# One-core two-layer trunk: the skip weights loaded as one row, a new order of the last rows, and three small moves in the projection blocks

## The chip, the cores and the metric

The kernel runs on one core of a Trainium2 chip. The metric is the device time of one execution in microseconds (us); lower is better. Five engines work side by side, each through its own instructions in program order: PE (TensorE, matrix products), DVE (VectorE), ACT (ScalarE), POOL (GpSimd) and SP (SyncE, which here only issues DMA transfers). They wait for each other through semaphores.

## The reference

The input is `x` of 1024 tokens by 1024 features, all float32. Two layers, each `h = h + W_out(mixer(rmsnorm(h)) * silu(z))`, then a last RMSNorm. Layer A mixes tokens within chunks of 128 by learned causal weights; layer B is a Mamba-2 state-space mixer with 32 heads. Cut to what matters here:

```python
def spatial_gating_mixer(h, w_in, ln_w, ln_b, w_s, b_s, w_out):     # layer A
    z, u, v = jnp.split(h @ w_in, 3, axis=-1)                       # 1024 -> 3 x 2048
    v = layernorm(v, ln_w, ln_b)
    mixed = jnp.einsum('gts,bcsgd->bctgd', w_causal, v) + b_s ...   # 8 groups, chunks of 128
    return (u * mixed * jax.nn.silu(z)) @ w_out

def ssd_mixer(h, w_in, conv_w, conv_b, dt_bias, a_log, d_skip, norm_w, w_out):   # layer B
    z, xbc, dt_raw = ...                                            # of h @ w_in
    xbc = silu(causal_depthwise_conv(xbc, conv_w, conv_b))
    dt = jax.nn.softplus(dt_raw + dt_bias)
    dA_cs = jnp.cumsum(dt * -jnp.exp(a_log), axis=2)
    ...                                                             # scan over 8 chunks
    y = y_diag + y_off + x * d_skip[..., None]                      # one skip weight a head
    gated = rmsnorm_by_group(y * jax.nn.silu(z))
    return gated @ w_out

h = h + mixer(rmsnorm(h, norm_w[i]), ...)                           # i = 0: A, i = 1: B
return rmsnorm(h, final_norm_w)
```

## The kernel before

Every large product is split into three products of rounded halves (`mm3`, lines 134 to 136: high by high, low by high, high by low), and two by two blocks of tokens and features are multiplied with seven block products in place of eight (Strassen's scheme, numbers 1 to 7 in the code). So weights have to be added to each other before they are used. ACT copies a sum into a rounded half `wh` or `xh` (line 111), DVE takes the rest into `wl` or `xl` (line 112), PE multiplies, and ACT copies some accumulators out (`u`, line 297). The order of all of this is written out by hand: the text of the program is the order on each engine. SBUF tiles come from small pools of a fixed number of buffers, taken in turn; who takes a buffer waits for its last user.

The run has these stages, with the times of the profile:

- Head (0 to about 190 us). `head()` normalises `x` and makes the first half of layer A's `v` columns, `rest()` the second half. Finished pieces of `v` lie in tiles `vt` of a pool of four 2 KB buffers (`k2`) and are stored to DRAM as `v_d` (line 397), by SP in the first half, by POOL in the second. Between them stand small loads on SP's queue: `hv` (lines 831 and 833, a bias and `a_log`) and the skip weights `dsk` (line 837), which layer B needs from about 1008 us on. `dsk` holds on partition `f * 64 + ...` the weights of the heads `2c + f`; the load takes every second weight of `b_d_skip`, once for each of 64 partitions. In `rest()`, `mix_a` masks layer A's mixing weights on POOL (line 861), `mix_b` transposes them on PE (869) and copies them on ACT into two `wc` tiles (871), which come from the same four `k2` buffers as `vt`, and `mix_c` multiplies `wc` by ones on PE (877).
- Layer A (to about 660 us): eight groups, then the output product.
- Projection blocks of layer B (about 640 to 1000 us): `into_b()` and `blocks()`. A block of 512 columns runs its seven products in units of 12 matmuls. `Block.sums_a` and `sums_b` build the two sums `t1` and `t2` in two halves of one tile: ACT writes minus a loaded block (lines 212, 218), and POOL's accumulating DMAs add further blocks from DRAM (line 203). `t2` feeds product 6, which comes third, and `fourth()` (line 228); `t1` feeds product 5, which comes fifth. Between the units stands `decays()`, a generator: each `yield` in it moves what follows to the next unit. It computes the time steps and their sums, with two exponentials on ACT (lines 1590 and 1620), stores them, spreads the last column of each chunk over 128 columns (`last`, line 1635), and has PE transpose them (1643) into `tk`.
- Scan and output product of layer B (about 1000 to 1447 us).
- End: `into_end()`. Rows of tokens are called (th, tt): th = 1 is the second half, ready first; th = 0 the first half, for which `last_mm(tt)` still runs 24 matmuls a row. `prep_unit` makes the operands of one `last_mm` (two `wh` on ACT, two `wl` on DVE). For a row of th = 0: `post` adds the product to the row on DVE (line 1232) and sums its squares on ACT (1251), `rstd_a` scales on DVE (1265) and takes a power on POOL (141), `rstd_b` refines on DVE (148, 152, 153), `finish_b` scales the left 512 columns on ACT (2201) and the right 512 on DVE (2203, together with the final norm weight `fnwb`), and two DMAs store them (2202, 2204). The left columns were weighed beforehand (2209).

Of the kernel before, what the change touches and what calls it, by code (L numbers as in the profile page):

```python
# [8 lines left out]
F32 = mybir.dt.float32  # L9
F32R = mybir.dt.float32r  # L10
AF = mybir.ActivationFunctionType
ALU = mybir.AluOpType
# [3 lines left out]
P = 128  # L16
# [13 lines left out]
def kernel(  # L30
# [21 lines left out]
    nc = tc.nc  # L52
    x = x[0]
    out = out[0]
# [3 lines left out]
    cst = ctx.enter_context(tc.tile_pool(name="cst", bufs=1))  # L58
# [6 lines left out]
    def s8(shape, name, dt=F32):  # L65
        return sb.tile(shape, dt, name=name, tag="s8", bufs=16)

    def q4(shape, name):
        return sb.tile(shape, F32, name=name, tag="q4", bufs=8)

    def k2(shape, name, dt=F32):
        return sb.tile(shape, dt, name=name, tag="k2", bufs=4)

    def k1(shape, name):
        return sb.tile(shape, F32, name=name, tag="k1", bufs=3)
# [21 lines left out]
    def sm(name):  # L97
        return ps[0].tile([P, 512], F32, name=name, tag="sm", bufs=n_sm[0])
# [84 lines left out]
    class Block:  # L183
# [32 lines left out]

        def sums_b(self):
            nc.scalar.mul(self.t1, self.b[0, 0], -1.0)
            self.add(self.t1, 0, 1)
            self.add(self.t2, 1, 1)  # L220

        def fourth(self):

# [604 lines left out]
    with tc.manual_schedule():  # L828
        second = head()
        hv = cst.tile([P, 4], F32, name="hv")  # L830
        nc.sync.dma_start(out=hv[0:32, 0:1], in_=b_dt_bias[0].rearrange("(h o) -> h o", o=1))
        for q in range(4):
            nc.sync.dma_start(out=hv[q * 32:(q + 1) * 32, 1:2], in_=b_a_log[0].rearrange("(h o) -> h o", o=1))
        dsk = cst.tile([P, 16], F32, name="dsk")
        dskv = b_d_skip[0].rearrange("(c f) -> f c", f=2)
        for f in range(2):
            nc.sync.dma_start(out=dsk[f * 64:(f + 1) * 64, :], in_=dskv[f].partition_broadcast(64))
        nA = hv[:, 2:3]
        nc.scalar.activation(nA, hv[:, 1:2], AF.Exp)
        nc.vector.tensor_scalar(nA, nA, -1.0, None, ALU.mult)  # L840
# [94 lines left out]
    for g in range(G):  # L935
        v = s8([P, NT, 256], "v")
# [645 lines left out]
    def decays():  # L1582

        dtw = q4([P, 4, 256], "dtw")
        cs = q4([P, 256], "cs")
        e_, s_, s2, p_ = (dtw[:, i, :] for i in range(4))
        V.scalar_tensor_tensor(e_, dtr, -1.0, dtr, ALU.mult, ALU.min)
        yield
        yield
        nc.scalar.activation(e_, e_, AF.Exp)  # L1590
        yield
        V.tensor_scalar(s_, e_, 2.0, None, ALU.add)
        V.reciprocal(s_[:, 0:P], s_[:, 0:P])
        yield
        V.reciprocal(s_[:, P:], s_[:, P:])
        V.tensor_tensor(s_, s_, e_, ALU.mult)
        V.tensor_tensor(s2, s_, s_, ALU.mult)
        yield
        V.tensor_scalar(p_, s2, 1.0 / 17, None, ALU.mult)
        for k in range(7, 0, -1):  # L1600
            if k in (5, 2):
                yield
            V.scalar_tensor_tensor(p_, p_, 1.0 / (2 * k + 1), s2, ALU.add, ALU.mult)
        V.scalar_tensor_tensor(p_, p_, 1.0, s_, ALU.add, ALU.mult)
        V.tensor_scalar(s2, dtr, 0.0, None, ALU.max)
        yield
        dt = dtr
        V.scalar_tensor_tensor(dt, p_, 2.0, s2, ALU.mult, ALU.add)
        dA = dtw[:, 0, :]
        V.tensor_scalar(dA, dt, nA, None, ALU.mult)  # L1610
        for j in range(2):
            V.tensor_tensor_scan(cs[:, j * P:(j + 1) * P], ones, dA[:, j * P:(j + 1) * P], 0.0, ALU.mult, ALU.add)
        yield
        dte = dtw[:, 2, :]
        for j in range(2):
            V.tensor_scalar(dte[:, j * P:(j + 1) * P], cs[:, j * P:(j + 1) * P], cs[:, j * P + P - 1:j * P + P], -1.0,
                            ALU.subtract, ALU.mult)
        yield
        ecs = dtw[:, 1, :]
        nc.scalar.activation(ecs, cs, AF.Exp)  # L1620
        nc.scalar.activation(dte, dte, AF.Exp)
        yield
        for q in range(4):
            rs_ = slice(q * 32, (q + 1) * 32)
            nc.gpsimd.dma_start(out=cs_d[2 * q:2 * q + 2].rearrange("c h l -> h c l"),
                              in_=cs[rs_, :].rearrange("h (c l) -> h c l", c=2))
            nc.gpsimd.dma_start(out=ecs_d[:, q * 256:(q + 1) * 256], in_=ecs[rs_, :])
            if q % 2:
                yield
        tk = s8([P, 2048], "tk")  # L1630
        tok = tk[:, 0:768].rearrange("p (v c r) -> p v c r", v=3, c=2)
        decb = tk[:, 768:1024]
        last = k1([P, 256], "last")
        for j in range(2):
            nc.scalar.copy(out=last[:, j * P:(j + 1) * P],
                           in_=ecs[:, j * P + P - 1:j * P + P].broadcast_to([P, P]))
        tps = []
        for two in ((dt, dte), (cs, last)):
            tp = sm("tp")
            tps.append(tp)  # L1640
            for i, src in enumerate(two):
                for j in range(2):
                    nc.tensor.transpose(out=tp[:, (2 * i + j) * P:(2 * i + j + 1) * P],
                                        in_=src[:, j * P:(j + 1) * P], identity=ident)
            yield
        nc.scalar.copy(out=tok[:, 0:2], in_=tps[0].rearrange("p (v c r) -> p v c r", v=2, c=2))
        yield
        nc.scalar.copy(out=tok[:, 2], in_=tps[1][:, 0:256].rearrange("p (c r) -> p c r", c=2))
        nc.scalar.copy(out=decb.rearrange("p (q j h) -> p j q h", q=4, j=2),
                       in_=tps[1][:, 256:512].rearrange("p (j q h) -> p j q h", j=2, q=4))  # L1650
        tok_of.update(tok=tok, decb=decb)
# [158 lines left out]
    def blocks():  # L1810
# [8 lines left out]
        bs[-1].apart = True  # L1819
        seq = [(k, n) for k in range(len(bs)) for n in (ORDER if k < len(bs) - 1 else LAST)]  # L1820
        small, turn, a21, done = decays(), [0], rest_a21(), []

        def ahead(at):
# [296 lines left out]
    def accs_b(n):  # L2120
        if n == 1:
# [3 lines left out]
    bo = Out(gd, b_w_out, gscale, lambda t, nb: h1_d[t][:, nb * 512:(nb + 1) * 512], accs_b, False,  # L2125
             (1, 2, 7, 6, 4, 5, 3))
    end = {}
# [68 lines left out]
            if c == 3:  # L2196
                bo.prep_unit(0)

    def finish_b(th, tt, rs):
        l, r = bo.row(th, tt, 0), bo.row(th, tt, 1)  # L2200
        nc.scalar.activation(l, l, AF.Identity, scale=rs)
        (nc.scalar if (th, tt) == (0, 3) else nc.sync).dma_start(out=outr[th * 4 + tt][:, 0:512], in_=l)
        nc.vector.scalar_tensor_tensor(r, r, rs, end["fnwb"][:, 512:], ALU.mult, ALU.mult)
        nc.sync.dma_start(out=outr[th * 4 + tt][:, 512:], in_=r)

    def weigh_left(th, t0):
        for tt in range(t0, t0 + 2):
            r = bo.row(th, tt, 0)
            nc.vector.tensor_tensor(out=r, in0=r, in1=end["fnwb"][:, 0:512], op=ALU.mult)  # L2209
# [221 lines left out]
    def into_end():  # L2431
        for n in (2, 7, 6, 4, 5):
            for _ in bo.product(n, hook_b):
                pass
        bo.prep_unit(1)
        weigh_left(1, 2)
        r1 = bo.rstd_half(1)
        for tt in range(4):
            bo.last_mm(tt)
            if 0 < tt < 3:  # L2440
                bo.prep_unit(tt + 1)
            if tt:
                bo.post(3, tt - 1)
                bo.rstd_a(0, tt - 1)
            finish_b(1, tt, r1[:, tt:tt + 1])
            if tt:
                finish_b(0, tt - 1, bo.rstd_b(0, tt - 1))
        bo.post(3, 3)
        bo.rstd_a(0, 3)
        finish_b(0, 3, bo.rstd_b(0, 3))  # L2450

    with tc.manual_schedule():
        scans()
        into_end()
# [28 lines left out]
```

## Time and profile before

| | us |
|---|---|
| median of 3 runs | 1481.93 (1481.75 to 1485.11) |
| the profiled execution | 1481.93 |
| its span, first to last instruction | 1480.2 |
| PE busy | 1452.0 (98%) |
| DVE busy | 1041.8 (70%) |
| ACT busy | 784.1 (53%) |
| POOL busy | 404.5 (27%) |

The profiled execution took the median's time; 1.73 us of it lie outside the span. Times in the profile count from the span's start. In a row of a timeline stand the start, the duration, the engine, the line, the operation with what it writes and reads, the count, and in brackets the engine's idle time before it with what ended that. PEq, SPq and so on are the sequencers that issue. In a list of waits stand who waited for whom, the sum in us, how often, and the longest.

### The profile page before, as it was taken

To read this page: it belongs to the slowest core of one execution; us is meant where nothing else is said; L and a number is where in the kernel's file an instruction comes from. 1 tells how busy PE (TensorE), PEld (TensorE's weight loads), DVE (VectorE), ACT (ScalarE), POOL (GpSimd) and SP (SyncE) were. 2 spreads that over 40 slices of the span, in tenths; PEclk is the share of its full clock that TensorE was granted. 3 is DMA by queue.
4 is the path that set the end of the run, shared out by engine and by line. 5 is a ranking of instruction groups with operands and counts; after the bars stand their busy time and mean duration, and the time that the engine had idled before them with its cause. 6 is when DMAs were issued, how large, how long until landed. Compare 5 with 4: busy or idle time off the path is not lost. (4 is left out here: it accounts for less than half of the span.)

```text
span 1480.2 us, 20005 instructions
## 1 busy us (share of the span) xinstructions
PE 1452.0 (98%) x7202; PEld 1196.5 (81%) x7202; DVE 1041.8 (70%) x1713; ACT 784.1 (53%) x1261; POOL 404.5 (27%) x451
## 2 busy tenths in 40 slices
PE   9998999999999999999999999999999999999997
PEld 7786888888888888887788888888888888787875
DVE  7864666776666655678665558767787777788976
ACT  7632333222323445565665646657677766866463
POOL 2101110000000023202122323205676767742221
PEclk9999999999999999999999999999999999999999
DMA  8653423332322999957467988786777566699963
GB/s 287 128 171 91 165 91 120 105 120 94 116 85 78 341 265 252 258 132 175 120 159 169 197 163 162 156 248 158 203 185 201 176 190 141 192 282 282 271 115 114
DMA packets 174549, 257.52 MB, mean 174 GB/s; under 512 B 16513, under 2 KB 98673, under 8 KB 171250
## 3 DMA queue, kind: packets, MB, share of 16 engines
q1 hardware_dynamic: 124128, 171.55, 37.7%
q0 software_dynamic: 42688, 70.79, 24.2%
q10 hardware_dynamic: 7634, 13.90, 2.6%
q8 instruction: 57, 0.93, 0.3%
q14 instruction: 42, 0.34, 0.1%
HBM read 187.19 MB, written 51.18 MB: 161 GB/s over the span
## 5 line engine op out<-in xcount | busy, mean ns | idle before, releaser
L134 PE MATMUL acc<-hh,wh 128*128 128x512 f32 x868 | 339.7, 391 | 0.7 <-ACT u L297 0.7
L136 PE MATMUL acc<-hh,wl 128*128 128x512 f32 x868 | 338.3, 390 | 0.4 <-DVE wl L112 0.3
L135 PE MATMUL acc<-hl,wh 128*128 128x512 f32 x868 | 337.8, 389 | 0.0
L136 PEld LDWEIGHTS acc<-hh,wl 128*128 128x128 f32 x868 | 162.9, 188 | 35.7 <-DVE wl L112 1.6
L134 PEld LDWEIGHTS acc<-hh,wh 128*128 128x128 f32 x868 | 163.1, 188 | 34.3 <-ACT u L297 1.1
L135 PEld LDWEIGHTS acc<-hl,wh 128*128 128x128 f32 x868 | 163.0, 188 | 33.0
L112 DVE TENSOR_TENSOR wl<-wr,wh 128x1024 fp32r<-128x1024 f32 (+1 forms) x81 | 96.2, 1188 | 105.8 <-ACT wh L111 105.6
L111 ACT CAST wh<-wr 128x1024 fp32r<-128x1024 f32 (+1 forms) x97 | 99.3, 1025 | 78.7 <-PE acc L135 58.7
L297 ACT COPY u<-acc 128x512 f32<-128x512 f32 x93 | 53.9, 582 | 148.0 <-PE acc L136 147.9
L134 PE MATMUL ab<-hh,wh 128*128 128x512 f32 x288 | 122.2, 424 | 0.0
L136 PE MATMUL ab<-hh,wl 128*128 128x512 f32 x288 | 113.2, 393 | 0.0
L135 PE MATMUL ab<-hl,wh 128*128 128x512 f32 x288 | 112.5, 391 | 0.6 <-DVE hl L112 0.6
L134 PE MATMUL acc<-wh,hh 128*128 128x512 f32 x216 | 85.6, 396 | 0.3 <-DVE vt L396 0.3
L135 PE MATMUL acc<-wl,hh 128*128 128x512 f32 x216 | 84.3, 390 | 1.0 <-DVE wl L364 1.0
L136 PE MATMUL acc<-wh,hl 128*128 128x512 f32 x216 | 84.1, 389 | 0.0
L976 POOL DMA_DIRECT2D y_d<-y x8 | 4.4, 550 | 287.2 <-DVE y L973 287.2
L1949 ACT ACTIVATE wl<-wl,tk 128x128 f32<-128x128 f32 x256 | 81.6, 392 | 0.3 <-DMA wl<-cs_d 0.2
L1967 DVE TENSOR_TENSOR wl<-wl,cw 128x512 f32<-128x512 f32 x64 | 61.0, 965 | 16.2 <-ACT wl L1951 15.1
L112 DVE TENSOR_TENSOR xl<-ya,xh 128x1024 fp32r<-128x1024 f32 x36 | 44.8, 1243 | 37.6 <-ACT xh L111 32.4
L1162 PE MATMUL bo<-wl,xh 128*128 128x512 f32 x192 | 64.2, 392 | 1.3 <-DVE stats L1253 0.7
L134 PEld LDWEIGHTS ab<-hh,wh 128*128 128x128 f32 x288 | 54.4, 189 | 13.3 <-issue 5.7
L111 ACT CAST xh<-ya 128x1024 fp32r<-128x1024 f32 x36 | 37.7, 1048 | 49.8 <-PE ao L1162 35.0
(331 smaller groups left out, 3236.4 us busy)
## 6 DMA issues: line engine op xcount, KB each, us to landing
wr<-in_a_w_in_dram SPq DMA_DIRECT2D x32, 512.0 KB, 3.6
wl<-cs_d SPq DMA_DIRECT2D x64, 256.0 KB, 5.4
wr<-in_b_w_in_dram SPq DMA_DIRECT2D x30, 512.0 KB, 4.3
wb<-in_a_w_out_dram SPq DMA_DIRECT2D x10, 1024.0 KB
wb<-in_b_w_out_dram SPq DMA_DIRECT2D x10, 1024.0 KB, 9.4
wr<-in_b_w_in_dram SPq DMA_DIRECT2D x36, 256.0 KB, 5.3
wide<-in_a_w_in_dram SPq DMA_DIRECT2D x16, 512.0 KB, 7.3
v<-v_d SPq DMA_DIRECT2D x8, 1024.0 KB
```

Source lines behind the costliest of these rows:

```text
L111: nc.scalar.copy(out=hi, in_=src)
L112: return (eng or nc.vector).tensor_tensor(out=lo, in0=src, in1=hi.bitcast(F32), op=ALU.subtract)
L134: nc.tensor.matmul(out=o, lhsT=l[0], rhs=r[0], start=start, stop=False, **kw)
L135: nc.tensor.matmul(out=o, lhsT=l[0], rhs=r[1], start=False, stop=False, **kw)
L136: nc.tensor.matmul(out=o, lhsT=l[1], rhs=r[0], start=False, stop=stop, **kw)
L297: nc.scalar.copy(out=self.u[n][:, i], in_=a)
L976: store = lambda: nc.gpsimd.dma_start(out=y_d[-1], in_=y)
L1162: nc.tensor.matmul(out=o[i], lhsT=X[x_][:, k, i * P:(i + 1) * P], rhs=Y[y_][:, k, :], start=not more and c == 0 and k == 0 and x_ == y_, s ...
L1949: nc.scalar.activation(wl[:, j, :], wl[:, j, :], AF.Relu, scale=-1.0, bias=tokc(2, c, self.g)[:, j:j + 1])
L1967: V.tensor_tensor(out=wl, in0=wl, in1=self.cw[c][:, 640:768].unsqueeze(1).broadcast_to([P, 4, P]), op=ALU.mult)
```

## The change

Five edits, in four places:

1. The skip weights come as one row of 32 values (`skip`, 128 bytes on each of 128 partitions) with one DMA in place of two, and DVE picks every second value with two copies of 64 partitions by 16.
2. `sums_b` adds to `t2` before it adds to `t1`.
3. In `decays()`, the first exponential (and all behind it) comes a unit later; the copies `last` stand a `yield` ahead of the transposes, which so come two units later than before.
4. The end is written out row by row: `prep_unit` comes ahead of the `finish_b` that stood before it, and `finish_b(1, 2)` after the sums of row (0, 1).
5. For the very last row the right half is weighed by `fnwb` (`left`) while the squares are summed, and DVE then only scales it.

```diff
@@ Block.sums_b
             nc.scalar.mul(self.t1, self.b[0, 0], -1.0)
+            self.add(self.t2, 1, 1)
             self.add(self.t1, 0, 1)
-            self.add(self.t2, 1, 1)
@@ behind head()
+        skip = cst.tile([P, 16, 2], F32, name="skip")
+        nc.sync.dma_start(out=skip.rearrange("p c f -> p (c f)"), in_=b_d_skip[0].partition_broadcast(P))
         dsk = cst.tile([P, 16], F32, name="dsk")
-        dskv = b_d_skip[0].rearrange("(c f) -> f c", f=2)
         for f in range(2):
-            nc.sync.dma_start(out=dsk[f * 64:(f + 1) * 64, :], in_=dskv[f].partition_broadcast(64))
+            nc.vector.tensor_copy(out=dsk[f * 64:(f + 1) * 64, :], in_=skip[f * 64:(f + 1) * 64, :, f])
@@ decays()
         yield
         yield
+        yield
         nc.scalar.activation(e_, e_, AF.Exp)
...
-        tk = s8([P, 2048], "tk")
-        tok = tk[:, 0:768].rearrange("p (v c r) -> p v c r", v=3, c=2)
-        decb = tk[:, 768:1024]
         last = k1([P, 256], "last")
         for j in range(2):
             nc.scalar.copy(out=last[:, j * P:(j + 1) * P],
                            in_=ecs[:, j * P + P - 1:j * P + P].broadcast_to([P, P]))
+        yield
+        tk = s8([P, 2048], "tk")
+        tok = tk[:, 0:768].rearrange("p (v c r) -> p v c r", v=3, c=2)
+        decb = tk[:, 768:1024]
@@ finish_b
-        nc.vector.scalar_tensor_tensor(r, r, rs, end["fnwb"][:, 512:], ALU.mult, ALU.mult)
+        if weighed is None:
+            nc.vector.scalar_tensor_tensor(r, r, rs, end["fnwb"][:, 512:], ALU.mult, ALU.mult)
+        else:
+            nc.vector.tensor_scalar(r, weighed, rs, None, ALU.mult)
@@ into_end()
-        for tt in range(4):
-            bo.last_mm(tt)
-            if 0 < tt < 3:
-                bo.prep_unit(tt + 1)
-            if tt:
-                bo.post(3, tt - 1)
-                bo.rstd_a(0, tt - 1)
-            finish_b(1, tt, r1[:, tt:tt + 1])
-            if tt:
-                finish_b(0, tt - 1, bo.rstd_b(0, tt - 1))
+        bo.last_mm(0)
+        bo.prep_unit(2)
+        bo.last_mm(1)
+        bo.post(3, 0)
+        bo.rstd_a(0, 0)
+        finish_b(1, 0, r1[:, 0:1])
+        bo.prep_unit(3)
+        finish_b(0, 0, bo.rstd_b(0, 0))
+        bo.last_mm(2)
+        bo.post(3, 1)
+        finish_b(1, 1, r1[:, 1:2])
+        bo.rstd_a(0, 1)
+        finish_b(1, 2, r1[:, 2:3])
+        finish_b(0, 1, bo.rstd_b(0, 1))
+        bo.last_mm(3)
+        bo.post(3, 2)
+        bo.rstd_a(0, 2)
+        finish_b(1, 3, r1[:, 3:4])
+        finish_b(0, 2, bo.rstd_b(0, 2))
         bo.post(3, 3)
+        left = k2([P, 512], "left")
+        nc.vector.tensor_tensor(out=left, in0=bo.row(0, 3, 1), in1=end["fnwb"][:, 512:], op=ALU.mult)
         bo.rstd_a(0, 3)
-        finish_b(0, 3, bo.rstd_b(0, 3))
+        finish_b(0, 3, bo.rstd_b(0, 3), left)
```

The engines' own order shows three of the places. In it the line numbers are those of each program; behind line 834 the changed one counts one to seventeen more.

SP's queue behind the last store of the first half, before, and then changed (`dsk` and `skip` are the skip weights; `64x16x1` is a transfer of single values):

```order
L863 DMA bsb<-in_a_b_s_dram 128x1024
L397 DMA v_d_79<-vt 256x1x256
L831 DMA hv<-in_b_dt_bias_dram 32x1
L833 DMA hv<-in_b_a_log_dram 32x1 x4
L837 DMA dsk<-in_b_d_skip_dram 64x16x1 x2
L937 DMA v<-v_d_78 128x2048
```

```order
L864 DMA bsb<-in_a_b_s_dram 128x1024
L397 DMA v_d_79<-vt 256x1x256
L831 DMA hv<-in_b_dt_bias_dram 32x1
L833 DMA hv<-in_b_a_log_dram 32x1 x4
L835 DMA skip<-in_b_d_skip_dram 128x32
L938 DMA v<-v_d_78 128x2048
```

Two transfers became one at the same place of the queue; the queue's other rows stand as they did. DVE's two copies of `skip` stand between the statistics of the second and the third piece of `v` of `rest()`.

ACT around the first exponential of `decays()` (`dtw`), before, and then changed:

```order
L297 COPY u<-acc 128x512
L1348 ACTIVATE zt<-zt 128x512
L1590 ACT_TABLE_LOAD
L1590 ACTIVATE dtw<-dtw 128x256
L111 CAST wh<-t_5546 128x1024
L297 COPY u<-acc 128x512 x2
L212 ACTIVATE t_5671<-wr 128x1024
```

```order
L297 COPY u<-acc 128x512
L1349 ACTIVATE zt<-zt 128x512
L111 CAST wh<-t_5548 128x1024
L297 COPY u<-acc 128x512
L1592 ACT_TABLE_LOAD
L1592 ACTIVATE dtw<-dtw 128x256
L297 COPY u<-acc 128x512
L212 ACTIVATE t_5670<-wr 128x1024
```

The table load and the exponential moved behind the cast `wh` and the first of the two copies `u`.

DVE in the end, from the norm of the second half (`rh`) to the finish of row (0, 0), before, and then changed (`wl` is `prep_unit`, `u<-bo,u` is `post`, `u<-u,rh,fnwb` a finish of th = 1, `u<-u,stats,fnwb` one of th = 0):

```order
L153 TENSOR_TENSOR rh<-rr,ru 128x4
L2203 SCALAR_TENSOR_TENSOR u<-u,rh,fnwb 128x512
L112 TENSOR_TENSOR wl<-ya,wh 128x512 x2
L1232 TENSOR_TENSOR u<-bo,u 128x512
L1265 SCALAR_TENSOR_TENSOR stats<-stats 128x1
L2203 SCALAR_TENSOR_TENSOR u<-u,rh,fnwb 128x512
L148 SCALAR_TENSOR_TENSOR ru<-rr,stats 128x1
L152 TENSOR_SCALAR ru<-ru 128x1
L153 TENSOR_TENSOR stats<-rr,ru 128x1
L2203 SCALAR_TENSOR_TENSOR u<-u,stats,fnwb 128x512
L112 TENSOR_TENSOR wl<-ya,wh 128x512 x2
L1232 TENSOR_TENSOR u<-bo,u 128x512
```

```order
L153 TENSOR_TENSOR rh<-rr,ru 128x4
L112 TENSOR_TENSOR wl<-ya,wh 128x512 x2
L1233 TENSOR_TENSOR u<-bo,u 128x512
L1266 SCALAR_TENSOR_TENSOR stats<-stats 128x1
L2207 SCALAR_TENSOR_TENSOR u<-u,rh,fnwb 128x512
L112 TENSOR_TENSOR wl<-ya,wh 128x512 x2
L148 SCALAR_TENSOR_TENSOR ru<-rr,stats 128x1
L152 TENSOR_SCALAR ru<-ru 128x1
L153 TENSOR_TENSOR stats<-rr,ru 128x1
L2207 SCALAR_TENSOR_TENSOR u<-u,stats,fnwb 128x512
L1233 TENSOR_TENSOR u<-bo,u 128x512
L2207 SCALAR_TENSOR_TENSOR u<-u,rh,fnwb 128x512
```

The first finish left the place ahead of the first pair `wl`, and the second pair `wl` went ahead of the refinement of row (0, 0).

More of the change, by code (lines that the diff above doesn't have):

```diff
@@ L2197, in hook_b, with finish_b @@
                 bo.prep_unit(0)
-    def finish_b(th, tt, rs):
+    def finish_b(th, tt, rs, weighed=None):
         l, r = bo.row(th, tt, 0), bo.row(th, tt, 1)
```

## Prediction, made before the changed kernel ran

> **What bounds the kernel now.** I read the page first, for the engine that is full:
>
> ```profile
> span 1480.2 us, 20005 instructions
> PE 1452.0 (98%) x7202; PEld 1196.5 (81%) x7202; DVE 1041.8 (70%) x1713; ACT 784.1 (53%) x1261; POOL 404.5 (27%) x451
> ```
>
> PE is busy for all but 28.2 us. None of the edits takes a matmul away, so only those 28.2 us can shrink: the waits inside, and the tail behind the last matmul. The second view is therefore the list of PE's waits, which begins:
>
> ```profile
> PE tp L877 <- ACT wc L871: 6.8, 1, 6.8
> ```
>
> This one wait is a quarter of all idle time. The third view is the timeline around it, for PE, ACT and POOL, and for SP's queue:
>
> ```profile
> 132.94 0.39 PE L135 MATMUL acc<-wl,hh 128*128 128x512 f32 x1
> 133.16 0.39 PE L136 MATMUL acc<-wh,hl 128*128 128x512 f32 x1
> 140.39 3.73 PE L877 MATMUL tp<-wc,ones 128*128 128x512 f32 x4 [6.84 <-ACT wc L871]
> 144.19 0.40 PE L135 MATMUL acc<-wl,hh 128*128 128x512 f32 x1
> 139.75 1.23 ACT L871 COPY wc<-tp 128x512 f32<-128x512 f32 x2 [20.62 <-DMA v_d<-vt]
> 119.60 0.73 POOL L397 DMA_DIRECT2D v_d<-vt  x1 [3.23 <-DVE vt L396]
> 117.40 1.40 SPq L837 DMA_DIRECT2D dsk<-in_b_d_skip_dram  x2
> ```
>
> PE waits for the copies `wc`, and ACT, in front of them, waits 20.62 us for stores of `v_d`: `wc` takes the `k2` buffers of `vt`, which are free when the stores have landed. POOL issued the first of them at 119.60. Why do they land 19 us later? The DMA view of the stretch 119 to 137 us, in the words of its summary, of a queue and of an issue:
>
> ```profile
> DMA packets 1927, 0.01 MB, mean 0 GB/s; under 512 B 1927, under 2 KB 1927, under 8 KB 1927
> q1 hardware_dynamic: 1927, 0.01, 4.7%
> v_d<-vt POOLq DMA_DIRECT2D x4, 256.0 KB, 19.1
> ```
>
> In those 18 us the DMA engines moved 0.01 MB in 1927 packets, all of SP's queue (q1), and not one packet of POOL's stores. The skip weights are 2 x 64 x 16 = 2048 single values, issued at 117.40: they are these packets, 18 us / 1927 = 9.3 ns each. The stores' 1 MB started when they were through.
>
> **The change part by part.**
>
> *Skip weights.* Removed: 2048 packets; added: one DMA of 128 rows of 128 bytes at the same place, and two DVE copies. At 9.3 ns a packet the row costs 1.2 us of DMA time beside a landing, for which the nearest row is the small load just ahead. The rows that bear on the rest are the usual landing of POOL's stores, the transposes that `wc` copies and DVE's last work before the gap:
>
> ```profile
> v_d<-vt POOLq DMA_DIRECT2D x16, 256.0 KB, 3.2
> hv<-in_b_a_log_dram SPq DMA_DIRECT2D x4, 0.1 KB, 2.1
> 127.06 1.03 PE L869 MATMUL tp<-ident,ws 128*128 128x128 f32 x8
> 124.19 2.34 DVE L356 TENSOR_TENSOR wide<-wide 128x1024 f32<-128x1024 f32 x2
> ```
>
> The row is issued at 117.40, so it is there by about 121, and DVE reaches the copies at about the same time, two pieces of `v` ahead of the row at 124.19. The copies have no row of their own size; no copy of 64 by 16 lasts longer than the 1.2 us of one of 128 by 1024, and DVE has cover: it is done with this stretch at 126.5 and next needed for a `wl` of 1.2 us for the product behind L877, by 135.1 as it comes out below, so 7.4 us. On SP's queue behind it stand only the loads of the next stage, for which buffers are not yet free, so one issue less is worth nothing. The stores, issued from 119.60 on, then land in their usual 3.2 us, the first two before 125; `wc` then waits only for the transposes of line 869, which end at 128.1. So L877 starts one matmul step (0.22, from 132.94 to 133.16) behind 133.16, at 133.4. How long do its four passes take? Here the clock had dropped:
>
> ```profile
> 139.00:141.00 2.00, 0.61 (x1) 0.50 (x2) 0.00 (x0) 1.19 (x3) 0.37 (x1) 0.50 0.76 234
> 1025.44 0.59 PE L1986 MATMUL os<-cw 128*128 128x256 f32 x2
> L1986 PE MATMUL os<-cw x112: 377/377/454, 1005.3 to 1315.3; 128*128 128x256 f32 x112
> ```
>
> The first row's third figure from the end is the granted clock, 0.50, after the idle stretch; the second is the same kind of product at full clock: two passes of 256 columns end 0.59 us after the start, and the third gives 377 ns for one, so they follow each other by 0.21 us, and passes of 512 columns by 0.43. Four take 1.7 us, and the second matmul behind them starts at 133.4 + 1.7 + 0.2 = 135.3 in place of 144.19. Gain 8.9 us, of which I take 8.8: the wait, and 2 us of half clock. Its ends: 0 if the stores still land late, 8.9 if nothing else is late. I stay near the upper end, since ACT and DVE have only work there that this wait held back: ACT's cast for the product behind L877 stands right behind `wc`.
>
> Here the Trainium skill speaks against me. "DMA: Bandwidth & Descriptors", section "Queues, rings and completion order", says that each DMA engine goes round-robin between the queues that have work, packet by packet. By that rule POOL's packets would have gone between the small ones and landed long before 137, the small packets would not be the cause, and this term would be 0. The trace disagrees: 1927 packets of one queue and none of the other in 18 us. I follow the trace and keep the rule as a rival.
>
> *Exponential a unit later.*
>
> ```profile
> 746.64 1.28 ACT L1590 ACT_TABLE_LOAD   x1
> 748.25 1.03 ACT L111 CAST wh<-t 128x1024 fp32r<-128x1024 f32 x1
> 749.19 1.06 ACT L297 COPY u<-acc 128x512 f32<-128x512 f32 x2
> 749.82 0.50 PE L134 MATMUL acc<-hh,wh 128*128 128x512 f32 x1 [0.69 <-ACT u L297]
> ```
>
> PE waits for the first copy `u`, behind table load, exponential and cast. With the two moved behind it, the cast runs at 746.64 and the copy ends near 748.2, before PE asks at 749.1. The second copy then ends at about 750.5; PE needs it a unit (12 matmuls, 2.7 us by the step above) after 749.1. Gain 0.7; the ends are 0 and the row's 0.69 with a slow restart, 0.85. All that follows in `decays()` has a unit of slack, and the order of the convolutions behind it stays.
>
> *Spread columns.*
>
> ```profile
> 778.38 0.53 PE L1643 MATMUL tp<-ident,last 128*128 128x128 f32 x2 [0.35 <-ACT last L1635]
> ```
>
> The copies `last` now run a unit ahead of the transposes, so this wait goes: gain 0.35, ends 0 and 0.35.
>
> *Two sums swapped.* This edit has two signs. First a block whose columns come in two pieces, then one in one piece, on POOL and ACT:
>
> ```profile
> 834.61 5.77 POOL L203 DMA_DIRECT2D t<-in_b_w_in_dram  x4
> 856.17 1.05 ACT L111 CAST wh<-t 128x1024 fp32r<-128x1024 f32 x1 [5.35 <-DMA t<-in_b_w_in_dram]
> 858.54 0.50 PE L136 MATMUL acc<-hh,wl 128*128 128x512 f32 x1 [0.26 <-DVE wl L112]
> 861.62 1.05 ACT L111 CAST wh<-t 128x1024 fp32r<-128x1024 f32 x1
> 755.80 1.27 POOL L203 DMA_DIRECT2D t<-in_b_w_in_dram  x1 [1.65 <-ACT t L218]
> 757.67 1.28 POOL L203 DMA_DIRECT2D t<-in_b_w_in_dram  x1 [0.59 <-DMA t<-in_b_w_in_dram]
> 785.43 1.07 ACT L111 CAST wh<-t 128x1024 fp32r<-128x1024 f32 x1
> ```
>
> In the first, four adds go out from 834.61 on, `t1` twice, then `t2` twice, and the cast of `t2` waits 5.35 us for the last of them; with `t2` ahead, it lands earlier by what the 512 KB of `t1` took, a few us, and PE's 0.26 goes: gain 0.25. In the last three rows `t2`'s add (757.67) waits on POOL until the earlier add to `t2` has landed. Put first, it waits as long, and `t1` goes out behind it, at about 759 in place of 755.80: 3 us later. In the two-piece block `t1` then is the last to land, near 856, and its cast is at 861.62, so 5 us of cover remain; in the one-piece block `t1`'s cast is the last row, 26 us behind the issue. Cost 0.
>
> *The end.* On PE, DVE, ACT and SP:
>
> ```profile
> 1469.86 0.39 PE L136 MATMUL bo<-yh,wl 128*128 128x512 f32 x1
> 1455.85 0.75 DVE L2203 SCALAR_TENSOR_TENSOR u<-u,rh,fnwb 128x512 f32<-128x512 f32 x1
> 1457.12 1.30 DVE L112 TENSOR_TENSOR wl<-ya,wh 128x512 fp32r<-128x512 f32 x2 [0.52 <-ACT wh L111]
> 1458.33 0.68 DVE L1232 TENSOR_TENSOR u<-bo,u 128x512 f32<-128x512 f32 x1
> 1464.24 0.68 DVE L1232 TENSOR_TENSOR u<-bo,u 128x512 f32<-128x512 f32 x1
> 1472.45 0.68 DVE L1232 TENSOR_TENSOR u<-bo,u 128x512 f32<-128x512 f32 x1
> 1475.49 0.72 ACT L2201 ACTIVATE u<-u,stats 128x512 f32<-128x512 f32 x1 [1.55 <-DVE stats L153]
> 1472.95 3.66 SPq L2204 DMA_DIRECT2D out_dram<-u  x2
> ```
>
> The last matmul ends at 1470.25, but the last row's `post` runs at 1472.45: not PE but the rows' own chain on DVE, ACT and POOL sets the end (from 1464.24 two rows take 8.21, 4.1 each). In the changed order the pair `wl` of row 2 runs at 1455.85, since ACT's casts no longer stand behind a finish, and the first `post` ends its wait at 1457.1, 1.2 earlier. From there to the next `post` was 5.9, of which the second pair `wl` (1.3) lay in the chain; now it lies in POOL's power of about 1.0 and its surroundings, and I count 5.3: 1462.4. Two more rows of 4.1 give 1470.6, against 1472.45: gain 1.85. Its ends: 1.2 if only the first shift holds, 2.1 where PE's 1470.25 becomes the bound. The weighed `left` shortens only DVE's last step; ACT's left half ends as late (1476.21 against 1476.25), and both stores leave together, so 0, at most 0.3.
>
> **Sum:** 8.8 + 0.7 + 0.35 + 0.25 + 1.85 = 11.95 us. The profiled execution took 1481.93, the median itself; 1481.93 - 11.95 = 1470.0.
>
> **The rivals.**
> 1. *The small packets are not the cause*, or the new row holds the stores as well. The gap stays, the other terms give 3.15: 1478.8. For it: the engines were 4.7% busy with these packets, so they were not full, and two queues served in turn would have let the stores by (this is what the Trainium skill's rule above says). Against it: the empty stretch, which ends with the small packets.
> 2. *Half the gap*: the stores land late for a second reason, or DVE waits for the row. A row that lands more than the 7.4 us late delays PE one for one; with half of 8.8 lost it is 1474.4. For it: no row shows such a broadcast's landing. Against it: the 2.1 us of the load ahead.
> 3. *Slower*: `t1` late. There are seven such blocks, and POOL holds `t1` 3.2 us (757.67 + 1.28 - 755.80). Once the cover of 5 us is gone, all seven cost PE; from (11.95 + 4.4) / 7 = 2.3 us a block on it ends slower, at 3.2 a block it is 1481.93 - 11.95 + 22.4 = 1492.4. Against it: the casts stand 5 us behind the landing in one kind of block, 26 us behind the issue in the other.
> 4. *The end gains nothing*, since DVE's order only trades one delay for another: 1471.9, inside my range.
>
> **How the numbers follow.** Forecast, with rival 4 and other small misses: 0.80, from 1467.5 (all upper ends, and some of the other waits) to 1473. Rival 2: 0.10. Rival 1: 0.07. Rival 3: 0.03. The range to hold 8 in 10 is 1467.5 to 1474.5, which takes in rival 2. A change under 0.3% (4.4 us) can't be told from none here; 1478.8 is 0.2% below, so "same" has rival 1 and "slower" rival 3, less a little of each for overlap: faster 0.91, same 0.07, slower 0.02.
>
> **What would show it.** Right: the list of PE's waits without the row of L877, stores of `v_d` by POOL all near 3 us, no granted clock of 0.50 behind 130 us; no PE wait for `u` or `last` near 750 and 778; the last `post` within 0.5 us of the last matmul's end; a span near 1468.3. Wrong: a wait of L877 that stays (rival 1), or a new one of DVE for `skip` (rival 2), or of PE or ACT for `t` in the blocks (rival 3).

## The result, and the profile after

The changed kernel takes 1468.06 us (median of 5 runs, 1466.58 to 1469.32) against 1481.93 before: a ratio of 0.9901, 95% interval 0.9887 to 0.9916. A second set gave 1468.67 us and 0.9899 (0.9884 to 0.9914). On 1481.93 the ratio makes 1467.3 us, 14.7 less than before, where 11.95 were forecast. The absolute medians lie in the predicted range of 1467.5 to 1474.5, 1.9 and 1.3 us below the forecast; the ratio's 1467.3 lies just under its lower end.

The page, and the first rows of the list of PE's waits (who waited for whom, sum in us, count, longest):

```profile
span 1464.9 us, 20002 instructions
PE 1447.6 (99%) x7202; PEld 1194.9 (82%) x7202; DVE 1043.2 (71%) x1716; ACT 783.7 (53%) x1261; POOL 404.0 (28%) x451
```
```profile
PE nw L451 <- POOL ident masks.py:199: 1.4, 1, 1.4
PE ab L135 <- DVE hl L112: 1.2, 1, 1.2
PE acc L135 <- DVE wl L364: 0.9, 1, 0.9
```

PE's idle time fell from 28.2 to 17.3 us, and the wait of 6.8 us for `wc` is gone; no row has come in its place. The timeline at that place (L870, L872 and L878 are lines 869, 871 and 877 of before):

```profile
126.06 1.07 ACT L872 COPY wc<-tp 128x512 f32<-128x512 f32 x2 [8.37 <-PE tp L870]
...
131.54 0.40 PE L136 MATMUL acc<-wh,hl 128*128 128x512 f32 x1
131.78 1.88 PE L878 MATMUL tp<-wc,ones 128*128 128x512 f32 x4
...
133.10 0.79 PE L134 MATMUL acc<-wh,hh 128*128 128x512 f32 x1
...
133.73 0.40 PE L135 MATMUL acc<-wl,hh 128*128 128x512 f32 x1
```

ACT's copies wait for PE's transposes only, and L878 starts one step behind the matmul ahead of it. The second matmul behind it starts at 133.73, before at 144.19: 10.46 us earlier, of which 1.62 were there already at 130 us (they come from the head, see `after_again`), so 8.8 here. PE's starts below are compared in this way, each matmul with the same one of the other profile. The stores and the row, in the view of the DMA queues between 112 and 150 us, and the granted clock (third figure from the end) where it had been 0.50:

```profile
v_d<-vt POOLq DMA_DIRECT2D x4, 256.0 KB, 2.6
...
skip<-in_b_d_skip_dram SPq DMA_DIRECT2D x1, 16.0 KB, 3.2
```
```profile
139.00:141.00 2.00, 2.00 (x10) 1.67 (x9) 2.00 (x2) 0.87 (x1) 0.54 (x1) 1.00 0.93 381
```

In the two-piece block ACT's cast of `t2` now waits 1.20 us in place of 5.35, and PE behind it not at all:

```profile
840.22 1.05 ACT L111 CAST wh<-t 128x1024 fp32r<-128x1024 f32 x1 [1.20 <-DMA t<-in_b_w_in_dram]
```

And the end, on DVE (L1233 is `post`, L2465 the new `left`, L2209 its scaling):

```profile
1444.32 0.69 DVE L1233 TENSOR_TENSOR u<-bo,u 128x512 f32<-128x512 f32 x1
...
1449.49 0.68 DVE L1233 TENSOR_TENSOR u<-bo,u 128x512 f32<-128x512 f32 x1
...
1453.61 0.68 DVE L1233 TENSOR_TENSOR u<-bo,u 128x512 f32<-128x512 f32 x1
...
1457.70 0.68 DVE L1233 TENSOR_TENSOR u<-bo,u 128x512 f32<-128x512 f32 x1
1458.41 0.69 DVE L2465 TENSOR_TENSOR left<-u,fnwb 128x512 f32<-128x512 f32 x1
...
1460.75 0.49 DVE L2209 TENSOR_SCALAR u<-left,stats 128x512 f32<-128x512 f32 x1
```

PE's last matmul ends at 1457.63, and the last `post` starts 0.07 behind it; before it was 2.20 behind. From PE's end to the span's end it is 7.27 us in place of 9.95: 2.68 gained.

### The profile page after: what moved, and what is told of

Read it like the earlier page. It is cut to its first block, busy times and chain, and to the rows that moved or that the text cites. A ratio compares the mean times of both kernels' runs of the same rounds, so it can differ in the third digit from the quotient of the medians.

```text
span 1464.9 us, 20002 instructions
## 1 busy us (share of the span) xinstructions
PE 1447.6 (99%) x7202; PEld 1194.9 (82%) x7202; DVE 1043.2 (71%) x1716; ACT 783.7 (53%) x1261; POOL 404.0 (28%) x451
## 5 line engine op out<-in xcount | busy, mean ns | idle before, releaser
L134 PEld LDWEIGHTS acc<-hh,wh 128*128 128x128 f32 x868 | 163.1, 188 | 32.9
## 6 DMA issues: line engine op xcount, KB each, us to landing
wb<-in_a_w_out_dram SPq DMA_DIRECT2D x10, 1024.0 KB, 12.4
```

Of the source, the lines that this page charges most:

```text
L134: nc.tensor.matmul(out=o, lhsT=l[0], rhs=r[0], start=start, stop=False, **kw)
```

## The experiments

Each run has its own runs of the kernel before beside it; their medians were 1482.25 to 1483.55, and the ratios are to them.

### The skip weights alone (`row_alone`)

```diff
+        skip = cst.tile([P, 16, 2], F32, name="skip")
+        nc.sync.dma_start(out=skip..., in_=b_d_skip[0].partition_broadcast(P))
         for f in range(2):
-            nc.sync.dma_start(out=dsk[f * 64:(f + 1) * 64, :], in_=dskv[f].partition_broadcast(64))
+            nc.vector.tensor_copy(out=dsk[f * 64:(f + 1) * 64, :], in_=skip[f * 64:(f + 1) * 64, :, f])
```

> The kernel before with the skip weights' row (one DMA, two copies) and nothing else of the change. Theory (the 2048 small packets held the stores of v_d, and nothing else did): no PE wait for wc, stores of v_d land near 3 us, 8.8 us less than before, 1473.1. Rival (part of the 8.9 us that PE's starts show between the two traces came with another edit, or the gap moves on): 1475 to 1478, with a new wait of PE between 133 and 180 us.

Measured: 1471.59 us, ratio 0.9932 (0.9919 to 0.9944), which is 8.3 to 12.0 us less. The wait for `wc` is gone, the stores land in 2.6 us. PE's starts gain 8.9 us on before's at L877 and still have 8.5 of them at the end. So this edit is the larger part of the change, and the others' waits stand where they were:

```profile
PE acc L134 <- ACT u L297: 0.9, 1, 0.9
...
PE tp L1644 <- ACT last L1636: 0.5, 1, 0.5
```

### Half of the small packets (`half_dose`)

```diff
+        nc.sync.dma_start(out=skip..., in_=b_d_skip[0].partition_broadcast(P))
-        for f in range(2):
-            nc.sync.dma_start(out=dsk[f * 64:(f + 1) * 64, :], in_=dskv[f].partition_broadcast(64))
+        nc.sync.dma_start(out=dsk[0:64, :], in_=dskv[0].partition_broadcast(64))
+        nc.vector.tensor_copy(out=dsk[64:128, :], in_=skip[64:128, :, 1])
```

> The kernel before with half the small packets: the skip weights of the lower 64 partitions as 64 x 16 single values as before, the upper half from a row and one copy. Theory (every small packet holds the stores by 9 to 10 ns): the packets end some 9.5 us sooner, near 128, the stores land near 131, wc is copied by 132 and PE asks for it at 133.4, so the wait of PE is gone as a whole, up to 0.5 us, while the stores still take about 11 us to land: 1473.0. Rival 1 (the stores are late for another reason, or the queues take turns): landing 19 us and wait 6.8 as before, 1481.9. Rival 2 (the wait falls in proportion to the packets): wait 3.4, 1478.

Measured: 1472.56 us, 0.9941 (0.9924 to 0.9958). The stores' landing and ACT's copies:

```profile
v_d<-vt POOLq DMA_DIRECT2D x4, 256.0 KB, 10.5
```
```profile
129.84 0.59 ACT L873 COPY wc<-tp 128x512 f32<-128x512 f32 x1 [12.19 <-DMA v_d<-vt]
130.72 0.59 ACT L873 COPY wc<-tp 128x512 f32<-128x512 f32 x1 [0.29 <-DMA v_d<-vt]
```

The landing fell from 19.1 to 10.5 us, 8.6 for 1024 packets fewer, and yet the whole of PE's wait is gone: the second copy ends at 131.3, and PE starts on them at 132.0 without a wait. Both rivals fall: the packets are the cause, and what PE pays has a threshold.

### Twice the small packets (`double_dose`)

```diff
+        for f in range(2):
+            nc.sync.dma_start(out=dsk2[f * 64:(f + 1) * 64, :], in_=dskv[f].partition_broadcast(64))
```

> The kernel before with twice the small packets: a second load of the skip weights, in the same form, into a tile that nothing reads. Theory (9 to 10 ns a packet): the stores land 19 to 20 us later, after about 39 us, PE waits 26 to 27 us for wc in place of 6.8, and the time is 1501 to 1503. Rival (the stores wait for something else, or the queues take turns): wait 6.8, 1481.9.

Measured: 1482.44 us, 1.0003 (0.9993 to 1.0012). The theory's 1501 did not come. The reason is seen in the wait, the landings and SP's queue:

```profile
PE tp L880 <- ACT wc L874: 7.5, 1, 7.5
```
```profile
v_d<-vt POOLq DMA_DIRECT2D x4, 256.0 KB, 21.5
...
wcT_d<-wc POOLq DMA_DIRECT2D x2, 256.0 KB, 17.6
```
```profile
115.62 1.41 SPq L837 DMA_DIRECT2D dsk<-in_b_d_skip_dram  x2
117.06 11.27 SPq L840 DMA_DIRECT2D dsk<-in_b_d_skip_dram  x2
```

The first two loads are issued in 1.41 us, the second two in 11.27: SP could not hand them over at once, and POOL issued its stores from 117.8 on, ahead of most of them. The second 2048 packets then held what came behind them, the stores of `wcT_d` (17.6 us), for which PE does not wait. So the experiment put only a few of the added packets ahead of the stores, and does not speak against 9 to 10 ns a packet; `more_ahead2`, below, mends that.

### The stores on a third queue (`stores_act`)

```diff
-            B.out("C11", i, 2, 1, G_)
+            B.out("C11", i, 2, 1, nc.scalar)
```

> The kernel before with all its small packets, but the four stores of v_d that wc waits for issued from ACT's queue and not POOL's. Theory A (the DMA engines serve what was issued first, whatever the queue): the stores land after about 19 us again, the wait stays, 1482. Theory B (the small packets hold POOL's queue alone, and a third queue gets its turns): the stores land in 3 to 5 us, the wait goes, 1473, up to 1 us more where ACT, in issuing them, waits for DVE's sums.

Measured: 1482.04 us, 0.9998 (0.9989 to 1.0008).

```profile
PE tp L877 <- ACT wc L871: 6.7, 1, 6.7
```
```profile
v_d<-vt ACTq DMA_DIRECT2D x4, 256.0 KB, 16.6
```

Theory A: it is not POOL's queue that is held, but whatever is issued behind the small packets.

### Half as many packets more, ahead of everything (`more_ahead`)

```diff
         hv = cst.tile([P, 4], F32, name="hv")
+        nc.scalar.dma_start(out=dsk2[0:64, :], in_=...[0].partition_broadcast(64))
```

> The kernel before with half as many small packets again, 1024, put on ACT's queue (a tile that nothing reads), where ACT issues them within a microsecond of SP's own, ahead of the first store of v_d. Theory A (the DMA engines work off in order of issue what all queues hold, 9.4 ns a small packet): the stores land after about 29 us, PE waits 16.4 us for wc in place of 6.8, 1491.9. Theory B (each queue has a pace of its own, and the two sets run side by side): the stores land after 19 us, wait 6.8, 1482.3.

Measured: 1477.58 us, 0.9962 (0.9948 to 0.9976): faster than before, which neither theory gave. My placing was wrong: ACT issued the extra load at 112.90, not at 117, and SP its own 2048 packets only at 126.32, behind the first two stores:

```profile
hv<-in_b_a_log_dram SPq DMA_DIRECT2D x4, 0.1 KB, 10.3
dsk<-in_b_d_skip_dram SPq DMA_DIRECT2D x2, 4.0 KB, 20.7
```
```profile
120.46 0.73 POOL L397 DMA_DIRECT2D v_d<-vt  x1 [3.14 <-DVE vt L396]
121.83 0.71 POOL L397 DMA_DIRECT2D v_d<-vt  x1 [0.64 <-DVE vt L396]
129.70 0.69 POOL L397 DMA_DIRECT2D v_d<-vt  x1 [7.17 <-DVE vt L396]
```

ACT's 1024 packets held SP's small loads `hv` for 10.3 us; DVE waited for them, and PE 2.1 us for DVE. The 2048 packets came too late to hold the two stores whose buffers `wc` takes, and the wait for `wc` fell away. The same packets, issued some 9 us later, cost PE nothing.

### The same behind SP's load (`more_ahead2`)

```diff
         nc.scalar.activation(nA, hv[:, 1:2], AF.Exp)
+        nc.scalar.dma_start(out=dsk2[0:64, :], in_=dskv[0].partition_broadcast(64))
```

> The kernel before with half as many small packets again, 1024, on ACT's queue (a tile that nothing reads), now issued behind SP's 2048 and behind the exponential for which DVE waits, near 119.1 us, some 0.5 us ahead of the first store of v_d. Theory A (the DMA engines work off what was issued ahead, in all queues, at 9.4 ns a small packet): the stores land after 28 to 29 us in place of 19.1, PE waits 15 to 16.5 us for wc in place of 6.8, 1491 to 1493. Theory B (the small packets of two queues run side by side): stores after 19 us, wait 6.8, 1482 to 1483.5.

Measured: 1493.27 us, 1.0082 (1.0062 to 1.0102), as theory A has it. The wait, and the DMA queues between 119 and 136 us:

```profile
PE tp L879 <- ACT wc L873: 16.3, 1, 16.3
```
```profile
DMA packets 1821, 0.01 MB, mean 0 GB/s; under 512 B 1821, under 2 KB 1821, under 8 KB 1821
...
q1 hardware_dynamic: 1821, 0.01, 4.7%
...
v_d<-vt POOLq DMA_DIRECT2D x4, 256.0 KB, 28.4
```

1024 packets more make the landing 9.3 us longer (28.4 against 19.1), 9.1 ns each; with `half_dose` that is nearly a line through three points, 10.5, 19.1 and 28.4 us for 1024, 2048 and 3072 packets. ACT's packets, issued at 118.86, moved none in these 17 us: they did not run beside SP's. They moved when SP's were through, most of them ahead of POOL's stores (q0), which were issued behind them. Between 139 and 146 us:

```profile
q0 software_dynamic: 50, 0.16, 5.8%
q10 hardware_dynamic: 743, 0.00, 4.7%
```

### The small packets behind the stores (`behind`)

```diff
-        for f in range(2):
-            nc.sync.dma_start(out=dsk[f * 64:(f + 1) * 64, :], in_=dskv[f].partition_broadcast(64))
@@ mix_b, behind the stores of wcT_d
+        for f in range(2):
+            nc.scalar.dma_start(out=dsk[f * 64:(f + 1) * 64, :], in_=dskv[f].partition_broadcast(64))
```

> The kernel before with its 2048 small packets in the old form, but issued from ACT's queue behind the two copies wc and their stores, near 128 to 131 us. Theory (only what stands ahead of the stores holds them): stores of v_d land near 3 us, no wait of PE for wc, and the transfers behind the small packets land up to 19 us late (the stores of addb_d and the 1 MB load of v, which in the run with the double load came 20 us late without a wait of PE): 1473. Rival (these late transfers are waited for, or the stores of wc are held): 1475 to 1482.

Measured: 1472.79 us, 0.9929 (0.9913 to 0.9946), as much as `row_alone`.

```profile
v_d<-vt POOLq DMA_DIRECT2D x13, 256.0 KB, 2.6
...
addb_d<-ab POOLq DMA_DIRECT2D x2, 512.0 KB, 16.9
wcT_d<-wc POOLq DMA_DIRECT2D x2, 256.0 KB, 11.4
```

The 2048 packets are all there. ACT issued them at 126.27 and 127.00, behind the stores of `v_d` and beside those of `wcT_d` (POOL, from 126.71 on). They hold other stores, which land after 11 to 17 us and for which nobody waits. So the 9 us hung on where the load stood as much as on its form.

### The end alone (`end_alone`) and the change without `left` (`no_left`)

`end_alone` is the kernel before with the parts of the diff in `finish_b` and `into_end()`, cut here to one place of the new order:

```diff
+        bo.rstd_a(0, 1)
+        finish_b(1, 2, r1[:, 2:3])
+        finish_b(0, 1, bo.rstd_b(0, 1))
+        bo.last_mm(3)
...
```

`no_left` undoes one edit of the changed kernel:

```diff
-        left = k2([P, 512], "left")
-        nc.vector.tensor_tensor(out=left, in0=bo.row(0, 3, 1), in1=end["fnwb"][:, 512:], op=ALU.mult)
-        finish_b(0, 3, bo.rstd_b(0, 3), left)
+        finish_b(0, 3, bo.rstd_b(0, 3))
```

> The kernel before with the new order of the end and the weighed left tile, and nothing else of the change. Theory (the order brings the last post to the end of PE's last matmul, 2.1 us, and some 0.5 us lie behind the last post): 2.6 us less than before, 1479.3; PE's end to the span's end 7.3 us in place of 9.95. Rival (my step as forecast): 1.85, with 8.1 us behind PE's end, 1480.1.

> The changed kernel without the left tile: the last row's right half is scaled and weighed in one step, as before; the order of the end stays. Theory 1 (what is gained behind the last post is the left tile's): 0.5 us slower than the changed kernel, 1468.6, with 7.75 us from the last post's start to the end in place of 7.20. Theory 2 (as forecast: the left tile is worth nothing, and the 0.5 us are the spread of the last store): the same time, 1468.1, with the stretch anywhere between 7.2 and 7.8 us.

Measured: `end_alone` 1479.19 us, 0.9975 (0.9961 to 0.9988); `no_left` 1469.14 us, 0.9907 (0.9894 to 0.9921), which the times do not tell from the changed kernel. By the traces, `end_alone` has 7.63 us from PE's end (1469.97) to the span's (1477.6) where before had 9.95, and its last `post` comes 0.07 behind PE:

```profile
1470.04 0.68 DVE L1232 TENSOR_TENSOR u<-bo,u 128x512 f32<-128x512 f32 x1
```

So the order is worth 2.13 us (2.20 less 0.07). What lies behind the last `post`: 7.14, 7.20, 7.21 and 7.56 us in the four profiles with `left` (the changed kernel twice, `no_swap`, `end_alone`; mean 7.28), 7.53 to 7.97 in the ten without it (mean 7.78). `left` takes about 0.5 us off, with a spread of 0.4 in each group, and the groups touch: `end_alone` has 7.56 with it, `no_left` 7.53 without. That pair alone would not have shown it.

### The changed kernel with the sums in their old order (`no_swap`)

```diff
-            self.add(self.t2, 1, 1)
             self.add(self.t1, 0, 1)
+            self.add(self.t2, 1, 1)
```

> The changed kernel with the two sums of the blocks in their old order. Theory (the swap takes a PE wait of 0.26 us in the two-piece block, 0.41 by the two traces, and costs nothing): PE waits near 846 us again, 0.4 us slower, 1468.5. Rival (the swap also made the wait of PE for hl near 976, 0.6 us longer than before, since another sum lands last there): that wait goes back to 0.6 us, the two cancel, 1468.1.

Measured: 1469.51 us, 0.9905 (0.9891 to 0.9918), not to be told from the change by the time. The trace tells it, by ACT's cast of `t2` and PE's wait behind it:

```profile
844.67 1.05 ACT L111 CAST wh<-t 128x1024 fp32r<-128x1024 f32 x1 [5.92 <-DMA t<-in_b_w_in_dram]
```
```profile
PE acc L136 <- DVE wl L112: 0.5, 1, 0.5
```

Between 830 and 862 us on before's clock PE's starts lose 1.1 us against the changed kernel there; before loses 0.6. The three profiles with the swap (the changed kernel twice, `no_left`) take the same 31.5 us for this stretch, the eleven without it 31.7 to 32.9, 32.2 in the mean. PE's wait for `hl` near 977 is absent in this run, which fits neither text; the next two runs take that up.

### The exponential and the columns alone (`blocks_alone`)

```diff
         V.scalar_tensor_tensor(e_, dtr, -1.0, dtr, ALU.mult, ALU.min)
         yield
         yield
+        yield
         nc.scalar.activation(e_, e_, AF.Exp)
...      (and last ahead of a yield, tk and the transposes behind it)
```

> The kernel before with the exponential a unit later and the last columns a unit sooner, and nothing else of the change. Theory: PE's waits for u near 750 (0.69) and for last near 778 (0.35) go, 1.05 to 1.35 us less than before, 1480.7. Rival (a gain there is given back at the next wait, or comes as a longer wait for hl near 985): under 0.5 us, 1481.5 or more.

Measured: 1481.93 us, 0.9993 (0.9984 to 1.0001). The list of waits has no `last` any more, and of `u` and `hl`:

```profile
PE ab L135 <- DVE hl L112: 2.0, 1, 2.0
...
PE acc L134 <- ACT u L297: 0.2, 1, 0.2
```

Between 735 and 787 us PE's starts gain 0.9 us on before. In this execution the wait for `hl` (the low half of an operand) near 990 took 1.5 us more than before, so its own time (1483.77) hides the gain. The ratio gives 1.0 us (-0.1 to 2.4), which by itself does not tell theory from rival. The traces show the gain in its place: that stretch of PE takes 50.4 to 51.5 us (mean 51.0) in the five profiles with this edit and 52.0 to 53.0 (mean 52.4) in the nine without it. Before's 52.0 is among the quickest of the nine. Whether some of the gain is given back at `hl`, the next run takes up.

### The changed kernel once more (`after_again`)

No edit: the same program a second time.

> The changed kernel once more. Theory (PE's wait for hl near 977, between 0 and 2.0 us in the nine profiles so far, comes and goes from one execution to the next with the loads ahead of it): 1468 again, that wait anywhere from 0 to 2 us, and the tail from the last post to the end within 0.2 us of 7.20. Rival (the change sets that wait): 1.2 us again.

Measured: 1468.67 us, 0.9899 (0.9884 to 0.9914). The list of PE's waits, to be held against the changed kernel's first one above:

```profile
PE nw L451 <- POOL ident masks.py:199: 1.4, 1, 1.4
PE os L1998 <- DVE state L2016: 1.2, 1, 1.2
PE os L1989 <- DVE cw L2027: 0.9, 1, 0.9
```

The wait for `hl` is gone, in the same program. Over the 14 profiles it is anything between 0 and 2.0 us, with and without each edit, so the change alone does not set it. Whether the exponential's new place makes it longer on average stays open: its mean is 0.95 us in the five profiles with that edit and 0.34 in the nine without. In the changed kernel's first profile ACT waits there 1.42 us for a load `f` and 1.89 for a load `wr`. The head is the second thing that differs between two profiles of one program. Its 32 transposes (least, median and greatest duration in ns, then first and last start in us), in the changed kernel's first profile:

```profile
L460 PE MATMUL tp<-both,weighed x32: 274/276/377, 10.6 to 14.2; 128*128 128x128 f32 x32
```

and in this run:

```profile
L460 PE MATMUL tp<-both,weighed x32: 275/421/583, 10.6 to 16.3; 128*128 128x128 f32 x32
```

Before has the slower form for most of them (421 at the median of those up to 15 us, 352 over all 32), as have `end_alone`, `blocks_alone` and both `more_ahead` runs; the other eight have the quicker one. The first product behind them starts at 14.3 us in the eight and at 15.9 to 17.0 in the six. `double_dose` and `stores_act` have the quicker head with none of the change's edits. So 1.6 of the 15.3 us between the first two spans are not the change's.

## Why the prediction came out as it did

**Skip weights, 8.8 forecast, 8.8 measured** by the first pair (9.2 with the mean of the three profiles that have this wait as before has it: before, `blocks_alone`, `end_alone`). Cause, place, the landing of the stores (3.2 forecast, 2.6 measured), DVE's cover and the half clock all came as worked out: no wait for `skip`, no clock under 1.00 in the stretch. Rivals 1 and 2 are refuted by `row_alone`, `half_dose` and `more_ahead2`. The Trainium skill ("DMA: Bandwidth & Descriptors", section "Queues, rings and completion order") lets each DMA engine go round-robin between the queues that have work. The runs do not agree: three queues had work in `more_ahead2`, and for 17 us all packets were of one; a landing that grows by 8.6 and 9.3 us per 1024 packets is what an order of issue gives. Not quite strictly: in `double_dose`, `behind` and, from 140 us on, `more_ahead2` some large packets went through while small ones were still moving.

**Exponential and columns, 1.05 forecast.** Between 735 and 787 us the first pair of traces gains 1.4 in all, `blocks_alone` 0.9, and the means over all profiles differ by 1.5. Up to 752 us, which takes in the wait for `u`, the five profiles with the edit gain 0.8 to 1.0, about the upper end of 0.85 that I had named.

**Sums swapped, 0.25 forecast, 0.6 by the first pair, 0.7 by the means, 1.1 by `no_swap`.** The row of 0.26 was the wait in one execution; it depends on when the last add lands (the cast waits 5.35 us in that one, 5.92 in `no_swap`). Rival 3 did not happen: `t1`'s cast behind it shows no wait.

**The end, 1.85 forecast, 2.68 measured.** This is the step of the prediction that failed: the cause was right, the term was mis-sized, by more than any other. Shifted by 12.62 us to before's clock (1470.25 less 1457.63), the first `post` stands at 1456.94 (1457.1 forecast), the second at 1462.11 (1462.4), the last at 1470.32 (1470.6). The stretch that I counted as 5.3 took 5.17, and PE became the bound, so the order reached its upper end, 2.13. The other 0.5 are behind the last `post`, where I put `left` at 0, at most 0.3, because "both stores leave together". They no longer do. The work behind the last `post` is hardly shorter (3.77 us in place of 3.80), so the gain lies in the stores: DVE's half is ready at 1461.24 and ACT's at 1461.46, where before they were ready at 1476.25 and 1476.21, and the last work is followed by 3.4 us in place of 3.95. That two stores which start together take longer to finish fits this, but was not tried by itself, and in `end_alone`, with its two stores as far apart, 3.8 us follow the last work. So the cause of these 0.5 us stays open. Rival 4 is refuted.

**The sum.** By the first pair of traces: 8.8 + 1.4 + 0.6 + 2.7 = 13.5, against 11.95. By the means over all profiles with and without each edit: 9.2 + 1.5 + 0.7 + 2.7 = 14.0. So every term came out larger than forecast, the end by 0.8 and the three others by about 0.4 each, partly because I read them from one profile of before, in which these waits happened to be short. The ratio gives 14.7, with an interval of 12.4 to 16.7. Singly, the ratios give 10.1 for the row, 3.7 for the end and 1.0 for the two moves, 14.8 together without the swap, each with an interval 2.5 to 4 us wide: the parts add up, and the 0.7 us between the means and the ratio are inside what these times can tell. What fills them stays open. The lower end of the range was the other fault. 1467.5 allowed for the upper ends of the terms, 12.75 us with 0.3 for `left`, and 1.7 us more, and the ratio's 1467.3 lies 0.2 below it. Waits that come and go (0 to 2 us for `hl`, 1.6 in the head) were in no term.

## What to carry to other kernels

Look in the trace for stretches in which thousands of tiny packets move and nothing else does: here 2048 single values, 8 KB in all, made the stores behind them land after 19 us in place of 3. Either make them rows, or issue them behind what is waited for; either was worth 10 us here by the ratios, and removing half of them was enough. Terms of a few tenths of a microsecond are read from a second profile of the same program first, since single waits here came and went by up to 2 us.

## What the runs showed of the hardware

- 1024, 2048 and 3072 packets of 4 bytes delayed the stores issued behind them to 10.5, 19.1 and 28.4 us, although the records have the DMA engines 4.7% busy. What the engines do in the rest of the time, no run shows.
- The hold was not tied to one queue: stores on ACT's queue took 16.6 us behind SP's packets, SP's loads 10.3 behind ACT's.
- Of four loads of 1024 small packets issued in a row by SP, the first two were handed over in 1.41 us, the second two in 11.27. What held SP, no run shows.
- The head's 32 transposes ran at a median of 276 or of 421 ns in executions of the same program, with a granted clock of 1.00 in both.
